# Hyena butterflies in a two-layer hybrid encoder: filter transforms on VectorE and in the attention, the convolution begun beside the queries

## The chip, the core and the metric

The kernel runs on one core of one Trainium2 chip, in one launch. The metric is device microseconds from start to end of the program. A profiled execution gives, besides its time, a trace of every engine: TensorE (PE, with its weight loads as PEld), VectorE (DVE), ScalarE (ACT), GpSimd (POOL) and the queue of SyncE (SP), which only issues transfers.

## What is computed

The reference is an encoder of two layers on 1024 tokens of width 1024, in float32. Each layer has a token mixer, a cross-attention into 256 memory tokens and a mixture of 16 experts, each with its residual and LayerNorm. The change lies in the mixer, whose three groups share one input projection:

```python
def hybrid_mix(x, ...):
    proj = x @ w_in
    gq, gk, gv, hy_u, c_q, c_kv, k_r = jnp.split(proj, IN_SPLITS, axis=-1)
    ...
    out_a = blocked_attention(q, k, v, HEAD_DIM ** -0.5)       # 8 heads, 2 key heads
    ...
    x0, x1, hv = jnp.split(short_conv3(hy_u, hy_cw, hy_cb), 3, axis=-1)
    filt = hyena_filters(n_tok, ...)                           # from weights alone
    out_b = x0 * bidir_long_conv(hv * x1, filt, hy_bias)
    ...
    out_c = blocked_attention(q_c, k_c, v_c, ...)              # latent attention, 4 heads
    return jnp.concatenate([out_a, out_b, out_c], axis=-1) @ w_o

def bidir_long_conv(z, h, bias):
    zs = jnp.fft.rfft(z, n=2 * n_tok, axis=1)
    fs = jnp.fft.rfft(filt_circ, axis=0)
    y = jnp.fft.irfft(zs * fs, n=2 * n_tok, axis=1)[:, :n_tok]
    return y + z * bias
```

The filter's spectrum `fs` hangs on weights only; `zs` and `y` hang on the tokens.

## The kernel before, in words

Every product of two f32 matrices is made of three matmuls (`mm3`, L184 to L189) on operands split into a high and a low part: `split` (L173 to L176) lets ACT copy the high part (L175) and VectorE, or with `"p"` GpSimd, subtract the low part (L176). Work in SBUF goes through one pool of 41 buffers of 128x1024 f32 (`big`); PSUM has the pools S (two of 128x1024), T and O (two of 128x512 each). The orders of PE, ACT and DVE are those in which the program text issues the instructions; a scheduler orders the queues of GpSimd and SyncE. The program text interleaves generators with `next()`, and each `yield` is a place where another stream goes on.

A length-2048 real Fourier transform is made of matmuls with DFT tables (128x1024 of one residue class at a time) and of radix butterflies: sums and differences of whole 128x1024 or half 128x512 tiles, here named bf, then the four spectra (F of the filter, Z of the tokens, G of the product on its way back).

- `filter_spectra` (from L810) makes the filter spectra of **both** layers, at the start of the program: windows and DFT matmuls first, whose results are seven tiles X per layer (U and V), then butterflies (L908 to L918) and `radix` (L926 to L950, an operation itself at L931), which take VectorE and GpSimd in turn (`alt`), ScalarE's scaling of Q (L932) between them; each layer's four F are stored to DRAM (fd, L923). Its steps are pulled by `fill`, four to each of the eight latent tiles of layer 1's projection.
- That stretch of the projection (`in_proj`, called the latent stretch below) has 8 tiles of 24 matmuls of 416 columns into PSUM O, with weights wi split on ACT and DVE. Behind each tile VectorE has a few small operations (L373 to L375 the norm, L502, L508 and L510 the rotary part of the key); L508 is the last that reads the tile from PSUM.
- Then come six tiles of convolution inputs, the keys and values, and eight query tiles (the query stretch), with L466 the query transposes. Attention overlaps the last of them.
- `hyena` (L952 to L1077) is the convolution. It reloads the tokens' channels, makes four transposes (T, L974) and four DFT steps (D), the forward butterflies (L994 to L997 and `radix`), four products with F (L1010 to L1017), the inverse butterflies (L1024 to L1032 and `radix`), splits the four G with the low part abl on GpSimd (L1046 with L176), and runs the inverse DFT matmuls, transposes (L1057) and the gating. All its butterflies and products are GpSimd's. It takes its first step at projection step 18, and then one per attention iteration, for n = 3 to 57.
- `attention` has 96 iterations, two for each of 48 pairs of head and block: 64 of grouped-query attention, 32 of latent attention. In each PE makes scores S (L526), VectorE the row maximum (L529), ACT the exponentials (L535), PE transposes (L543), which ACT and VectorE split into PH and PL (L175, L176), and PE the output (L553, L554). After every second iteration ACT evicts olo (L565 to L567), of which there are two buffers, and GpSimd finishes it (L568, L569). `side(n, 2)` pulls the steps of other streams.

```python
            def side(n, at):
                ...
                if HY0 <= n < 58:
                    next(hy, None)
```

Of the kernel before, what the change touches and what calls it, by code (L numbers as in the profile page):

```python
# [11 lines left out]
F32 = mybir.dt.float32  # L12
# [7 lines left out]
D = 1024  # L20
# [12 lines left out]
TAIL = 88  # L33
ML0 = 1
FM = 14
HY0 = 3
AT0 = 14
UC = 1
UG = 3
# [98 lines left out]
class Net:  # L138
# [58 lines left out]
    def consts(self):  # L197
        nc, cp, A = self.nc, self.cp, self.A
        self.ident = cp.tile([128, 128], F32, name="ident")
        nc.sync.dma_start(self.ident, A["k_ident"])  # L200
        self.eps = cp.tile([128, 2], F32, name="eps")
        nc.vector.memset(self.eps[:, 0:1], 1e-6)
        nc.vector.memset(self.eps[:, 1:2], 1e-5)
        self.x1d = [self.dp.tile([N, D], F32, name=f"x1d{l}") for l in range(DEPTH)]
        self.x2d = [self.dp.tile([N, D], F32, name=f"x2d{l}") for l in range(DEPTH)]
        self.yd = [self.dp.tile([N, D], F32, name=f"yd{l}") for l in range(DEPTH)]
        self.x3d = self.dp.tile([N, D], F32, name="x3d")
        self.cd = [self.dp.tile([N, C_COLS], F32, name=f"cd{l}") for l in range(DEPTH)]
        self.kvd = [self.dp.tile([8, 128, 1024], F32, name=f"kvd{l}") for l in range(DEPTH)]
        self.ld = [self.dp.tile([20, 128, 1024], F32, name=f"ld{l}") for l in range(DEPTH)]  # L210
        self.zd = [self.dp.tile([4, 128, 1024], F32, name=f"zd{l}") for l in range(DEPTH)]
        self.fd = [self.dp.tile([4, 128, 1024], F32, name=f"fd{l}") for l in range(DEPTH)]

    def tables(self):
# [595 lines left out]
    def filter_spectra(self):  # L810
# [74 lines left out]
        for n in range(9):  # L885
# [18 lines left out]
            if n % 2 == 0 and n < 8:  # L904
                tab = nxt.pop()
                if n < 6:
                    nxt.append(self.table("k_dft", n // 2 + 1))
        for l in range(DEPTH):  # L908
            E, O, D, Od, Oe, Dd, Q = (self.big(sh, name="bf") for _ in range(7))
            u, v = U[l], V[l]  # L910
            for k, (o, a, b, op) in enumerate((
                    (E, u[0], u[1], OP.add), (O, u[2], u[3], OP.add), (Od, u[2], u[3], OP.subtract),
                    (Oe, v[1], v[2], OP.add), (Dd, v[1], v[2], OP.subtract),
                    (D[:, 0], u[0][:, 0], u[1][:, 0], OP.subtract), (D[:, 1], v[0][:, 0], v[0][:, 1], OP.subtract),
                    (Q[:, 0], Od[:, 0], Od[:, 1], OP.subtract), (Q[:, 1], Dd[:, 0], Dd[:, 1], OP.add))):
                self.alt().tensor_tensor(o, a, b, op)
                if k in (1, 3, 5, 8):
                    yield  # L918
            U[l] = V[l] = u = v = None
            F = [self.big(sh, name="F") for _ in range(4)]  # L920
            yield from self.radix(F, E, O, (Oe[:, 0], Oe[:, 1]), D, Q)
            for i in range(4):
                nc.sync.dma_start(self.fd[l][i], F[i].rearrange("p a b c -> p (a b c)"))  # L923
            yield

    def radix(self, F, E, O, b2, D, Q, pool=False):  # L926

        nc = self.nc  # L930
        tt = lambda *x: (nc.gpsimd if pool else self.alt()).tensor_tensor(*x)  # L931
        nc.scalar.activation(Q, Q, AF.Copy, scale=math.sqrt(0.5))  # L932
        S, AB = (self.big((128, 2, 2, 256), name="bf") for _ in range(2))
        tt(S[:, 0], E[:, 0], E[:, 1], OP.add)
        tt(S[:, 1], O[:, 0], O[:, 1], OP.add)
        yield
        tt(AB[:, 0], E[:, 0], E[:, 1], OP.subtract)
        tt(AB[:, 1], *b2, OP.subtract)
        yield
        tt(F[0][:, 0], S[:, 0], S[:, 1], OP.add)  # L940
        tt(F[0][:, 1], S[:, 0], S[:, 1], OP.subtract)
        yield
        tt(E, D, Q, OP.add)
        yield
        tt(O, D, Q, OP.subtract)
        yield
        for f, x in zip(F[1:], (AB, E, O)):
            for i, op in enumerate((OP.add, OP.subtract)):
                tt(f[:, i], x[:, 0], x[:, 1, ::-1], op)
            yield  # L950

    def hyena(self, l):  # L952
# [44 lines left out]
        tt(Q[:, 1], Od[:, 0], Od[:, 1], OP.add)  # L997
        del X[:]
        yield
        Z = [self.big(sh, name="Z") for _ in range(4)]  # L1000
        yield from self.radix(Z, E, O, (O[:, 0], O[:, 1]), D, Q, True)
        Y = []
        for i in range(4):
            F = self.big(sh, name="F")
            nc.sync.dma_start(F, self.fd[l][i].rearrange("p (a b c) -> p a b c", a=2, b=2))
            t1 = self.big(sh, name="y1")
            t2 = self.big(sh, name="y2")
            d = slice(None, None, -1 if i else 1)
            z, z2 = Z[i], t1[:, d, 1]
            tt(t1, z, F, OP.mult)  # L1010
            yield
            tt(t2[:, :, 0], z[:, :, 0], F[:, d, 1], OP.mult)
            tt(t2[:, :, 1], z[:, d, 1], F[:, :, 0], OP.mult)
            yield
            y = self.big(sh, name="y3")
            tt(y[:, :, 0], t1[:, :, 0], z2, OP.subtract)
            tt(y[:, :, 1], t2[:, :, 0], t2[:, :, 1], OP.add)  # L1017
            Y.append(y)
            yield
# [12 lines left out]
        tt(Q[:, 1], Od[:, 1], Od[:, 0], OP.subtract)  # L1032
        del Y
        yield
        G = [self.big(sh, name="G") for _ in range(4)]
        yield from self.radix(G, E, O, (O[:, 1], O[:, 0]), D, Q, True)
        for j in (4, 5):
            self.mix_dst(j * 128, 0, 1)
        zv = [reload(2 + i) for i in range(2)]
# [2 lines left out]
        for n in range(6):  # L1042
            if n < 4:
                ah = self.big(sh, F32R, name="abh")
                al = self.big(sh, F32R, name="abl")
                self.split(ah, al, G[n], "p")  # L1046
                tab = nxt.pop()
                if n < 3:
                    nxt.append(self.table("k_idft", n + 1))
                ready.append((n, ah, al, tab))  # L1050
                yield
            if late:
                q, t = late.pop()
                pt = self.psT((128, 2, 2, 128))
                for i in range(2):
                    for ct in range(2):
                        nc.tensor.transpose(pt[:, i, ct, :], t[:, i, ct * 128:ct * 128 + 128], self.ident)  # L1057
                a, b = INV[q]
                for ct in range(2):
                    for hf in range(2):  # L1060
                        s = slice(hf * 64, hf * 64 + 64)
                        w = slice(min(a, b), max(a, b) + 1, abs(b - a))
                        p = pt[:, :, ct, s] if a < b else pt[:, ::-1, ct, s]
                        dst = self.mix[hf][2][:, ct, :].rearrange("p (m r) -> p r m", r=8)[:, w, :]
                        nc.vector.tensor_tensor(dst, p, zv[ct][:, w, s], OP.mult)
                if n == 5:
                    yield
            if 0 < n < 5:
                q, ah, al, tab = ready.pop(0)
                P = self.psO((128, 2, 256))  # L1070
                for i in range(2):
                    for cs in range(2):
                        k = (i, cs) if q == 0 else (i ^ cs, cs)
                        self.mm3(P[:, i, :], tab[:, 0, i, cs, :], tab[:, 1, i, cs, :], ah[:, k[0], k[1], :], al[:, k[0], k[1], :], cs == 0, cs == 1)
                t = self.tmp((128, 2, 256), name="yt")
                nc.scalar.activation(t, P, AF.Copy)
                late.append((q, t))  # L1077
                yield
# [627 lines left out]
    def run(self):  # L1706
# [38 lines left out]
        for l in range(DEPTH):  # L1745
# [3 lines left out]
            wo = []  # L1749
            gqa, (mla, back) = self.gqa(), self.mla(l)  # L1750
            hy = self.hyena(l)

            def side(n, at):
                if at != 2:
                    return
                if HY0 <= n < 58:
                    next(hy, None)
                if n == 58:
                    drain(hy)
                if 57 <= n < 64 or n in (70, 78, 86):  # L1760
                    next(back, None)
                if n in (84, 86, 88, 90, 92, 94, 96, 97):
                    wo.extend(self.out_weights(A["w_o"][l], [len(wo)]))
# [3 lines left out]
            for n, _ in enumerate(proj, NT if l else 0):  # L1767
                if n == NT - 1 + (l > 0):
                    drain(mem if l else fill)
                if n == 18:  # L1770
                    next(hy)
                if AT0 + NT + 2 <= n:
                    next(att)
                    next(att)
                    ATS += 2
# [12 lines left out]
            for n, _ in enumerate(att, ATS):  # L1788
                if n == PS:
                    next(pl)  # L1790
            if PS > 101:
                next(pl)
            T1 = self.new_T()
# [123 lines left out]
def drain(g):  # L1917
    for _ in g:
        pass
# [63 lines left out]
```

## Time and profile before

| | before |
|---|---|
| median of 3 runs (lowest to highest) | 2769.97 us (2769.33 to 2772.05) |
| the profiled execution's own time | 2770.48 us |
| its span, first to last instruction | 2768.7 us |
| mean granted TensorE clock | 0.967 of full |
| PE busy | 2548.5 us, 92% |
| DVE busy | 1960.4 us, 71% |
| ACT busy | 1588.1 us, 57% |
| POOL busy | 872.8 us, 32% |

The two layers pass through the same stages, layer 2 some 1320 us behind layer 1; only the first has the filter's work. Layer 1's latent stretch lies at 135 to 195 us of the span, its grouped-query attention at 370 to 590, its latent attention at 590 to 693. A table of busy times by stretch of time is the way to read these stages apart: the shares over the whole span are averages of stages with different limits.

### The profile page before, as it was taken

To read this page: it belongs to the slowest core of one execution; us is meant where nothing else is said; L and a number is where in the kernel's file an instruction comes from. 1 tells how busy PE (TensorE), PEld (TensorE's weight loads), DVE (VectorE), ACT (ScalarE), POOL (GpSimd) and SP (SyncE) were. 2 spreads that over 40 slices of the span, in tenths; PEclk is the share of its full clock that TensorE was granted. 3 is DMA by queue.
4 is the path that set the end of the run, shared out by engine and by line. 5 is a ranking of instruction groups with operands and counts; after the bars stand their busy time and mean duration, and the time that the engine had idled before them with its cause. 6 is when DMAs were issued, how large, how long until landed. Compare 5 with 4: busy or idle time off the path is not lost. (4 is left out here: it accounts for less than half of the span.)

```text
span 2768.7 us, 39154 instructions
## 1 busy us (share of the span) xinstructions
PE 2548.5 (92%) x14132; PEld 2146.8 (78%) x14132; DVE 1960.4 (71%) x3066; ACT 1588.1 (57%) x2828; POOL 872.8 (32%) x784
## 2 busy tenths in 40 slices
PE   7879999899899995999989998989989999599998
PEld 5668878789778884777769887878977887477775
DVE  6775568677653478888977456877766347888887
ACT  4624259788323443778854425977841344278885
POOL 2473339932301300111132333994230121011112
PEclk9889999999999997999999999999999999799999
DMA  7436100142232356999975620114223234699994
GB/s 200 145 133 214 52 24 32 43 103 77 84 106 79 106 181 237 333 372 377 345 258 175 192 75 24 31 39 107 69 91 107 77 99 160 252 327 371 379 350 152
DMA packets 220563, 455.40 MB, mean 164 GB/s; under 512 B 26074, under 2 KB 82992, under 8 KB 220370
## 3 DMA queue, kind: packets, MB, share of 16 engines
q1 hardware_dynamic: 196386, 367.22, 37.9%
q0 software_dynamic: 19376, 68.91, 9.3%
q10 hardware_dynamic: 4608, 16.78, 1.5%
q8 instruction: 111, 1.82, 0.3%
q14 instruction: 82, 0.67, 0.1%
HBM read 366.08 MB, written 86.77 MB: 164 GB/s over the span
## 5 line engine op out<-in xcount | busy, mean ns | idle before, releaser
L176 DVE TENSOR_TENSOR egl<-eg,egh 128x1024 fp32r<-128x1024 f32 x256 | 305.9, 1221 | 49.7 <-ACT egh L175 45.2
L529 DVE TENSOR_REDUCE nm<-S 128x1 f32<-128x1024 f32 x192 | 234.4, 1223 | 109.2 <-PE S L526 108.1
L175 ACT ACTIVATE egh<-eg 128x1024 fp32r<-128x1024 f32 x256 | 265.2, 1058 | 40.9 <-PE S L188 23.8
L176 DVE TENSOR_TENSOR PL<-T,PH 128x512 fp32r<-128x512 f32 x384 | 246.2, 683 | 40.5 <-ACT PH L175 38.2
L175 ACT ACTIVATE PH<-T 128x512 fp32r<-128x512 f32 x384 | 209.2, 595 | 76.5 <-PE T L543 75.5
L543 PE MATMUL T<-ident,E 128*128 128x128 f32 x1536 | 205.8, 276 | 18.5 <-DVE PL L176 17.7
L543 PEld LDWEIGHTS T<-ident,E 128*128 128x128 f32 x1536 | 181.1, 142 | 50.1 <-DVE PL L176 22.8
L535 ACT ACTIVATE E<-S,nm 128x1024 f32<-128x1024 f32 x192 | 214.6, 1118 | 7.5 <-DVE nm L529 7.4
L187 PE MATMUL S<-woh,mh 128*128 128x512 f32 x512 | 207.5, 405 | 6.3 <-DVE r L1150 6.3
L188 PE MATMUL S<-wol,mh 128*128 128x512 f32 x512 | 202.2, 395 | 3.6 <-POOL wol L176 2.4
L187 PE MATMUL S<-egh,xt 128*128 128x512 f32 x512 | 204.1, 399 | 0.0
L189 PE MATMUL S<-woh,ml 128*128 128x512 f32 x512 | 201.6, 394 | 0.0
L189 PE MATMUL S<-egh,xt 128*128 128x512 f32 x512 | 200.7, 392 | 0.0
L188 PE MATMUL S<-egl,xt 128*128 128x512 f32 x512 | 200.6, 392 | 0.0
L176 DVE TENSOR_TENSOR edl<-ed,edh 128x1024 fp32r<-128x1024 f32 x128 | 153.2, 1220 | 18.5 <-ACT edh L175 18.5
L1658 PE MATMUL O<-edh,ht 128*128 128x512 f32 x512 | 155.3, 406 | 1.4 <-ACT ht L175 1.4
L568 POOL TENSOR_TENSOR olo<-olo 64x256 f32<-64x256 f32 x96 | 70.0, 729 | 269.4 <-ACT olo L566 267.7
L526 PE MATMUL S<-KS,QS 128*128 128x512 f32 x512 | 148.8, 415 | 1.2 <-ACT E L535 1.2
L1600 POOL DMA_INDIRECT xg<-x2d,ix x32 | 54.6, 1705 | 301.2 <-PE O L1658 143.1
L175 ACT ACTIVATE edh<-ed 128x1024 fp32r<-128x1024 f32 x128 | 132.3, 1055 | 22.9 <-PE S L188 13.2
L553 PE MATMUL O<-PH,VS 128*128 128x256 f32 x512 | 139.3, 305 | 0.0
L1673 POOL DMA_INDIRECT yd<-ye,ix x31 | 49.0, 1582 | 260.8 <-DVE egl L176 114.0
(423 smaller groups left out, 7148.8 us busy)
## 6 DMA issues: line engine op xcount, KB each, us to landing
eg<-moe_w_gate SPq DMA_DIRECT2D x128, 512.0 KB, 10.9
eg<-moe_w_up SPq DMA_DIRECT2D x128, 512.0 KB, 11.0
ed<-moe_w_down SPq DMA_DIRECT2D x128, 512.0 KB, 11.3
wv<-xa_wkv SPq DMA_DIRECT2D x16, 512.0 KB, 8.1
wk<-xa_wkv SPq DMA_DIRECT2D x16, 512.0 KB, 6.3
wo<-w_o SPq DMA_DIRECT2D x16, 512.0 KB, 3.5
x1d<-r SPq DMA_DIRECT2D x16, 512.0 KB, 2.6
wq<-xa_wq SPq DMA_DIRECT2D x16, 512.0 KB, 4.0
```

Source lines behind the costliest of these rows:

```text
L175: self.nc.scalar.activation(h, src, AF.Copy)
L176: (self.nc.vector if le == "v" else self.nc.gpsimd).tensor_sub(l, src, h.bitcast(F32))
L187: mm(out, ah, bh, start=start, stop=False)
L188: mm(out, ah, bl, start=False, stop=False)
L189: mm(out, al, bh, start=False, stop=stop)
L526: self.nc.tensor.matmul(S[:, hf * 512:hf * 512 + 512], a, b[hf], start=n == 0, stop=n == len(passes) - 1)
L529: self.nc.vector.tensor_reduce(nm, S, axis=AX.X, op=OP.max, negate=True)
L535: self.nc.scalar.activation(E, S, AF.Exp, bias=nm, scale=1.0, accum_out=den)
L543: self.nc.tensor.transpose(pt[:, k, :], P[:, kt * 128:(kt + 1) * 128], self.ident)
L553: nc.tensor.matmul(O[:, :256], v, PH[half][:, k, :], start=kt == 0, stop=False)
L568: nc.gpsimd.tensor_tensor(lo[s, 0], lo[s, 0], lo[s, 1], OP.add)
L1658: nc.tensor.matmul(O[e][n], a[:, 2 * u + f, :], w[:, n * 512:n * 512 + 512], start=s, stop=z)
```

## The change

Four things are done, and PE's instructions stay the same in number.

1. Layer 1's filter butterflies run in the latent stretch as before, but all on VectorE (`filter_radix` with `nc.vector`), with two yields a step.
2. Layer 2's seven X tiles are stored to DRAM (ud, 512 KB each) by SP, right after the DFT. In layer 1's latent attention, at odd n over 62, `filter_later` loads them back and makes the butterflies on GpSimd: 7 operations on 128x1024 and 16 on 128x512, one scaling on ACT, four stores to fd.
3. The convolution takes a step at each projection step from 18 to 26, which is beside the queries, and then one at each attention iteration below 58 save each sixth.
4. The low parts of the four inverse splits go from GpSimd to VectorE. `radix` now makes and hands on one spectrum at a time, and frees its inputs earlier.

```diff
-HY0 = 3
+        self.ud = self.dp.tile([7, 128, 1024], F32, name="ud")
...
+        for i, x in enumerate(U[1] + V[1]):
+            nc.sync.dma_start(self.ud[i], x.rearrange("p a b c -> p (a b c)"))
+        uv = dict(enumerate(U[0] + V[0]))
+        del U, V, x
+        for _ in self.filter_radix(0, uv.pop, nc.vector):
+            yield
+            yield
+
+    def filter_later(self):
...
+        xs = {i: load(i) for i in (2, 3)}
...
+        yield from self.filter_radix(1, get, self.nc.gpsimd)
+
+    def filter_radix(self, l, get, eng):
+        tt, sh = eng.tensor_tensor, (128, 2, 2, 256)
+        def two(i, j):
+            a, b = get(i), get(j)
+            o = self.big(sh, name="bf")
+            tt(o, a, b, OP.add)
+            yield
+            tt(a, a, b, OP.subtract)
+            yield
+            return o, a
...
-                self.split(ah, al, G[n], "p")
+                self.split(ah, al, G.pop(n))
...
+            later = self.filter_later()
...
-                if HY0 <= n < 58:
+                if n < 58 and n % 6 != 5:
                     next(hy, None)
                 if n == 58:
                     drain(hy)
+                if n > 62 and n % 2 and l == 0:
+                    next(later, None)
...
-                if n == 18:
+                if 18 <= n:
                     next(hy)
```

On VectorE, at the start of the latent stretch, the rows before are these (bf are butterfly tiles, X the DFT's results, cn and r the latent tile's norm and rotary part):

```order
L878 COPY X<-S 128x512
L176 TENSOR_TENSOR xl<-T,xh 128x2x256
L916 TENSOR_TENSOR bf<-X 128x1024 x3
L916 TENSOR_TENSOR bf<-X 128x512
L916 TENSOR_TENSOR bf<-bf 128x512
L373 RECIPROCAL ri<-sd 128x2
L375 SCALAR_TENSOR_TENSOR cn<-O,ri,mgq 128x256
```

and with the change:

```order
L942 TENSOR_TENSOR bf<-X 128x1024
L944 TENSOR_TENSOR X<-X 128x1024
L373 RECIPROCAL ri<-sd 128x2
L375 SCALAR_TENSOR_TENSOR cn<-O,ri,mgq 128x256
L375 SCALAR_TENSOR_TENSOR cn<-O,ri,mgk 128x128
L502 TENSOR_TENSOR r_1272<-O,rope_369 128x32
L508 TENSOR_TENSOR r_1274<-O,rope_369 128x2x8 x2
L510 TENSOR_TENSOR cn<-r_1272,r_1274 128x32
L942 TENSOR_TENSOR bf<-X 128x1024
L944 TENSOR_TENSOR X<-X 128x1024
```

Where five butterflies stood ahead of the first tile's norm, and others on GpSimd beside them, two stand ahead of it and two to four behind each tile, and none on GpSimd.

On GpSimd, from the end of the query stretch into the attention, the rows before (tab are DFT tables, t and xr the queries' rotary part):

```order
L287 TENSOR_TENSOR t_3226<-xn,rg 128x16x16 x2
L292 TENSOR_TENSOR xr<-xr,t_3226 128x512
L803 DMA tab<-k_dft 128x1024 x3
L568 TENSOR_TENSOR olo<-olo 64x256
L569 TENSOR_TENSOR mix<-olo 64x256
L568 TENSOR_TENSOR olo<-olo 64x256
L569 TENSOR_TENSOR mix<-olo 64x256
L568 TENSOR_TENSOR olo<-olo 64x256
L569 TENSOR_TENSOR mix<-olo 64x256
L994 TENSOR_TENSOR bf<-X 128x1024 x2
```

and with the change:

```order
L803 DMA tab<-k_dft 128x1024
L287 TENSOR_TENSOR t_3169<-xn,rg 128x16x16 x2
L292 TENSOR_TENSOR xr<-xr,t_3169 128x512
L287 TENSOR_TENSOR t_3236<-xn,rg 128x16x16 x2
L292 TENSOR_TENSOR xr<-xr,t_3236 128x512
L1042 TENSOR_TENSOR bf<-X 128x1024 x4
L1044 TENSOR_TENSOR bf<-bf 128x512
L1045 TENSOR_TENSOR bf<-bf 128x512
L978 TENSOR_TENSOR bf<-bf 128x512
L979 TENSOR_TENSOR bf<-bf 128x512
L568 TENSOR_TENSOR olo<-olo 64x256
```

The convolution's eight first operations stand ahead of the first eviction pair now, where the first two stood behind the third pair.

In SP's queue ahead of the latent stretch, before:

```order
L820 DMA dec<-hy_decay 128x512
L826 DMA hyb<-hy_bias 1x512
L1243 DMA kvd_88<-kk 128x1024 x2
L1739 DMA x<-x 128x1024 x8
L127 DMA wi<-w_in 128x2x416 x4
L377 DMA cd_86<-cn 128x416
L923 DMA fd_94<-F 128x1024
L647 DMA c<-cd_86 128x416
```

and with the change:

```order
L820 DMA dec<-hy_decay 128x512
L826 DMA hyb<-hy_bias 1x512
L1293 DMA kvd_88<-kk 128x1024 x2
L1789 DMA x<-x 128x1024 x4
L909 DMA ud<-X 128x1024
L1789 DMA x<-x 128x1024 x4
L909 DMA ud<-X 128x1024 x4
L126 DMA wi<-w_in 128x2x416 x4
L909 DMA ud<-X 128x1024 x2
```

Five of the seven stores stand ahead of the latent weights wi, and wait for their X tiles there.

## Rows read from the trace of the kernel before

**Rows 1.** Busy time by stretch: start:end, length, then each engine, clock, DMA.

```profile
135.00:195.00 60.00, 44.94 (x194) 41.87 (x194) 53.24 (x76) 14.81 (x49) 46.22 (x24) 0.86 0.38 128
369.00:412.00 43.00, 38.00 (x237) 32.91 (x238) 30.49 (x41) 28.60 (x54) 7.17 (x10) 0.88 0.11 37
...
502.00:520.00 18.00, 11.03 (x66) 9.53 (x65) 8.15 (x13) 10.85 (x22) 17.53 (x15) 0.81 0.00 0
520.00:560.00 40.00, 35.27 (x260) 32.21 (x258) 28.75 (x42) 34.34 (x69) 32.23 (x29) 1.00 0.26 80
...
590.00:693.00 103.00, 103.00 (x714) 93.47 (x713) 76.11 (x108) 83.47 (x171) 24.88 (x36) 1.00 0.24 71
```

**Rows 2.** The same view, of L529 alone: one row maximum per attention iteration.

```profile
457.00:502.00 45.00, 19.58 (x16) 1.00 0.07 25
502.00:520.00 18.00, 3.65 (x3) 0.81 0.00 0
520.00:560.00 40.00, 13.47 (x11) 1.00 0.26 80
```

**Rows 3.** Timeline of the latent stretch: start, length, instruction, [idle before, releaser].

```profile
140.15 0.35 PE L189 MATMUL O<-wih,xl 128*128 128x416 f32 x1
140.34 0.36 PE L187 MATMUL O<-wih,xh 128*128 128x416 f32 x1
...
149.41 0.69 PE L187 MATMUL O<-wih,xh 128*128 128x416 f32 x1 [4.93 <-DVE r L508]
```

**Rows 4.** Groups of DVE and of POOL, 135 to 195 us: count, busy, mean ns, idle.

```profile
L931 DVE TENSOR_TENSOR F<-bf 128x512 f32<-128x512 f32 x8 | 12.8, 1631 | 0.0
L510 DVE TENSOR_TENSOR cn<-r,r 128x32 f32<-128x32 f32 x7 | 6.1, 868 | 0.2
L375 DVE SCALAR_TENSOR_TENSOR cn<-O,ri,mgq 128x256 f32<-128x256 f32 x7 | 3.4, 484 | 0.7
L375 DVE SCALAR_TENSOR_TENSOR cn<-O,ri,mgk 128x128 f32<-128x128 f32 x7 | 2.4, 342 | 0.0
L931 DVE TENSOR_TENSOR bf<-bf 128x1024 f32<-128x1024 f32 x2 | 2.4, 1213 | 0.0
L508 DVE TENSOR_TENSOR r<-O,rope 128x16 f32<-128x16 f32 x14 | 1.7, 165 | 0.0
...
L916 POOL TENSOR_TENSOR bf<-X 128x1024 f32<-128x1024 f32 x5 | 13.7, 2752 | 10.9 <-issue 6.4 <-DVE bf L916 4.5
```

**Rows 5.** Groups of DVE in layer 2, 1450 to 1560 us, without butterflies.

```profile
L510 DVE TENSOR_TENSOR cn<-r,r 128x32 f32<-128x32 f32 x8 | 1.5, 192 | 0.3
```

**Rows 6.** Timeline ahead of the latent stretch: SP's, ACT's and DVE's queues.

```profile
115.94 3.66 SPq L127 DMA_DIRECT2D wi<-w_in  x4
...
123.70 0.89 ACT L175 ACTIVATE wih<-wi 128x832 fp32r<-128x832 f32 x1
...
120.49 0.68 DVE L878 COPY X<-S 128x512 f32<-128x512 f32 x1
```

**Rows 7.** Groups of POOL in the attention, 412 to 560 us.

```profile
L568 POOL TENSOR_TENSOR olo<-olo 64x256 f32<-64x256 f32 x22 | 16.1, 733 | 8.6 <-ACT olo L566 7.7
...
L931 POOL TENSOR_TENSOR Z<-bf 128x512 f32<-128x512 f32 x8 | 10.1, 1287 | 0.1
...
L931 POOL TENSOR_TENSOR bf<-bf 128x1024 f32<-128x1024 f32 x4 | 9.5, 2398 | 0.0
```

**Rows 8.** Timeline of POOL: the convolution's first butterflies.

```profile
415.10 4.73 POOL L994 TENSOR_TENSOR bf<-X 128x1024 f32<-128x1024 f32 x2
```

**Rows 9.** Timeline of ACT and of PE, later in the attention.

```profile
510.99 1.06 ACT L932 ACTIVATE bf<-bf 128x1024 f32<-128x1024 f32 x1 [5.58 <-POOL bf L1032]
...
542.62 0.36 PE L187 MATMUL O<-abh,tab 128*128 128x256 f32 x1 [2.56 <-ACT E L535]
```

**Rows 10.** Groups of DVE: 505 to 560 us, then 590 to 693.

```profile
L176 DVE TENSOR_TENSOR PL<-T,PH 128x512 fp32r<-128x512 f32 x28 | 18.1, 685 | 11.2 <-ACT PH L175 11.0
...
L176 DVE TENSOR_TENSOR PL<-T,PH 128x512 fp32r<-128x512 f32 x62 | 39.6, 681 | 0.0
```

More of the change, by code (lines that the diff above doesn't have):

```diff
@@ L907, in filter_spectra @@
                     nxt.append(self.table("k_dft", n // 2 + 1))
[L908 to L923, printed above, removed]
-            yield
@@ L926, in radix @@
[L926 to L933, printed above, removed]
+        for i, x in enumerate(U[1] + V[1]):
[3 more added lines that the diff above has]
+        for _ in self.filter_radix(0, uv.pop, nc.vector):
+            yield
+            yield
@@ new lines, in filter_later, with load, get @@
+    def filter_later(self):
+        def load(i):
+            x = self.big((128, 2, 2, 256), name="X")
+            self.nc.sync.dma_start(x, self.ud[i].rearrange("p (a b c) -> p a b c", a=2, b=2))
+            return x
+        xs = {i: load(i) for i in (2, 3)}
+        def get(i):
+            order = (2, 3, 5, 6, 0, 1, 4)
+            for j in order[:min(7, order.index(i) + 3)]:
+                if j not in xs:
+                    xs[j] = load(j)
+            x, xs[i] = xs[i], None
+            return x
+        yield from self.filter_radix(1, get, self.nc.gpsimd)
@@ new lines, in filter_radix, with store @@
+    def filter_radix(self, l, get, eng):
[8 more added lines that the diff above has]
+            return o, a
+        O, Od = yield from two(2, 3)
+        Oe, Dd = yield from two(5, 6)
+        Q = self.big(sh, name="bf")
+        tt(Q[:, 0], Od[:, 0], Od[:, 1], OP.subtract)
+        tt(Q[:, 1], Dd[:, 0], Dd[:, 1], OP.add)
+        del Od, Dd
+        yield
+        u, w = get(0), get(1)
+        E, D = self.big(sh, name="bf"), self.big(sh, name="bf")
+        tt(E, u, w, OP.add)
+        yield
+        tt(D[:, 0], u[:, 0], w[:, 0], OP.subtract)
+        del u, w
+        w = get(4)
+        tt(D[:, 1], w[:, 0], w[:, 1], OP.subtract)
+        del w
+        yield
+        def store(i, f):
+            self.nc.sync.dma_start(self.fd[l][i], f.rearrange("p a b c -> p (a b c)"))
+        yield from self.radix(store, E, O, Oe, (0, 1), D, Q, tt)
@@ L934, in radix @@
+    def radix(self, emit, E, O, Oe, b2, D, Q, tt):
+        sh = (128, 2, 2, 256)
+        self.nc.scalar.activation(Q, Q, AF.Copy, scale=math.sqrt(0.5))
+        S, AB = (self.big(sh, name="bf") for _ in range(2))
         tt(S[:, 0], E[:, 0], E[:, 1], OP.add)
@@ L937, in radix @@
         tt(AB[:, 0], E[:, 0], E[:, 1], OP.subtract)
[L938 to L941, printed above, removed]
+        tt(AB[:, 1], Oe[:, b2[0]], Oe[:, b2[1]], OP.subtract)
         yield
@@ L946, in radix @@
         yield
-        for f, x in zip(F[1:], (AB, E, O)):
+        f = self.big(sh, name="Z")
+        tt(f[:, 0], S[:, 0], S[:, 1], OP.add)
+        tt(f[:, 1], S[:, 0], S[:, 1], OP.subtract)
+        emit(0, f)
+        yield
+        for n, x in enumerate((AB, E, O)):
+            f = self.big(sh, name="Z")
             for i, op in enumerate((OP.add, OP.subtract)):
                 tt(f[:, i], x[:, 0], x[:, 1, ::-1], op)
+            emit(n + 1, f)
             yield
@@ L999, in hyena @@
         yield
-        Z = [self.big(sh, name="Z") for _ in range(4)]
-        yield from self.radix(Z, E, O, (O[:, 0], O[:, 1]), D, Q, True)
+        Z = {}
+        yield from self.radix(Z.__setitem__, E, O, O, (0, 1), D, Q, tt)
+        del E, O, D, Od, Q
         Y = []
@@ L1008, in hyena @@
             d = slice(None, None, -1 if i else 1)
-            z, z2 = Z[i], t1[:, d, 1]
+            z, z2 = Z.pop(i), t1[:, d, 1]
             tt(t1, z, F, OP.mult)
@@ L1034, in hyena @@
         yield
-        G = [self.big(sh, name="G") for _ in range(4)]
-        yield from self.radix(G, E, O, (O[:, 1], O[:, 0]), D, Q, True)
+        G = {}
+        yield from self.radix(G.__setitem__, E, O, O, (1, 0), D, Q, tt)
+        del E, O, D, Od, Q
         for j in (4, 5):
@@ L1790, in run @@
                     next(pl)
+            if l == 0:
+                drain(later)
             if PS > 101:
```

## The prediction

> **What bounds the kernel now.** I read the busy times by stretch first. TensorE sets the pace where it is busy throughout: in the latent attention, 590 to 693 us, it works 103.00 of 103 us, and nothing there can be won [rows 1]. It does not set it in four other stretches of layer 1 [rows 1]: the latent stretch (44.94 of 60 us busy, at 0.86 of the clock), the start of attention (38.00 of 43, 0.88), the 18 us from 502 (11.03, 0.81) and the 40 us from 520 (35.27). The timeline says who is late. In the latent stretch it is VectorE: PE stands 4.93 us for L508, the last read of a PSUM tile [rows 3], which queues behind butterflies. Their lengths by group show why: with both engines at it, a 128x512 butterfly takes VectorE 1.63 us, an addition of 32 columns 0.87, and a 128x1024 takes GpSimd 2.75 [rows 4]; in layer 2, without butterflies, the same 32 columns take 0.19 [rows 5]. In attention it is GpSimd: it is busy 17.53 of the 18 us from 502 [rows 1], and ACT stands 5.58 us with the scaling of Q, behind L1032 [rows 9]; everything after it in ACT's order, the exponentials among it, stands too.
>
> **Latent stretch, layer 1.** At full clock the matmuls follow each other in 0.19 us (140.15 to 140.34) [rows 3]. Eight tiles of 24 make 192 x 0.19 = 36.5 us; the stretch lasts 60.0, so at most 23.5 can go, stalls and half clock together. VectorE's work afterwards, all butterflies included: 7 x 1.21 [rows 4] and 16 of 128x512, for which I take the 0.68 that this size costs in attention [rows 10], 19.4 us or 2.4 a tile; its own operations 0.48 + 0.34 + 2 x 0.165 [rows 4] + 0.19 [rows 5], with two smaller ones some 1.7. Together 4.1 us, under PE's 4.56: PE becomes the bound, by a small margin. GpSimd has nothing left there, so nothing slows VectorE. Two things take from the 23.5. The weights wi are now issued behind five stores of X, of which the last waits for the copy that ends at 121.2; they were issued at 115.94 and first split at 123.70 [rows 6]. If they need all of those 7.8 us, the first split moves by 5.3; if they land sooner, by less, at the least by nothing. I take 3. For clock and hand-overs left I take 1.5. Gain 19, between 12 and 23.5.
>
> **Convolution in attention, both layers.** PE's steady pace is 16 iterations in 45 us, 2.81 each [rows 2]. The 18 us from 502 hold 3 iterations [rows 2], so 18 - 8.4 = 9.6 us are lost. They are a backlog: forward butterflies (14 x 1.29 + 6 x 2.40 = 32.5 us), products (4 x (2.40 + 4 x 1.29) = 30.2) and the inverse's first ones (some 12.5) by the lengths in [rows 7], with an eviction pair of 2 x 0.73 [rows 7] per two iterations (34 iterations, 25), make 100 us; GpSimd has 96 from its start at 415.10 [rows 8] to the end of the stall at 510.99 [rows 9]. With the change these steps begin some 40 us earlier (the first DFTs are beside the queries) and take five of six iterations: 41 iterations or 115 us for the same work plus pairs, 105. GpSimd is then in time, and the 9.6 go.
>
> At the start of attention PE idles 5.0 of 43 us and loses clock besides [rows 1]; five of the eight transpose and DFT steps leave it. Their PE work only moves, so I count 3 (0 to 5). In the 40 us from 520, PE idles 4.73 [rows 1]; one wait there is 2.56 before the first inverse DFT [rows 9]. The trace names the exponentials, but these were done; the other operand is the low part abl, which GpSimd makes. With abl on VectorE and the steps earlier I take 3.5 of the 4.73 (0 to 4.7).
>
> The moved low parts cost VectorE 4 x 1.21, and it has 40 - 28.75 = 11.25 us free there [rows 1], which hides them; if each also waits for a GpSimd operation of 2.40 [rows 7], as butterflies did in the latent stretch, it is 9.6 more, 3.2 over what is free. I take 1 (0 to 9.6). So a layer gives 9.6 + 3 + 3.5 - 1 = 15, and two 30, between 12 and 38. Layer 2 has the same PE work and nothing of the filter's.
>
> **Rule against row.** VectorE's PL, which reads one operand from PSUM, takes 0.685 us beside a busy GpSimd and 0.681 beside a mostly idle one [rows 10], whereas the butterflies with both operands in SBUF suffer [rows 4]. The Trainium skill, GPSIMD Engine Reference, section "1. Specifications", says that GpSimd shares its SBUF interfaces with VectorE, and that instructions of VectorE with two SBUF inputs contend. By that rule the low parts on VectorE, two SBUF inputs each, would contend every time, and the sum would be smaller by up to 17 us; the trace agrees with the rule on butterflies and on PL, and shows no low part on VectorE beside GpSimd.
>
> **Layer 2's filter, moved into layer 1's latent attention.** GpSimd gets 16 x 1.29 + 7 x 2.40 = 37.5 us [rows 7] on top of 24.88 in 103 us [rows 1]: room is ample. VectorE's work there is PL and maxima, both from PSUM, and is not slowed [rows 10]. The seven stores and loads of 512 KB and the four stores of F cost by what queues behind them: loads of latent-attention keys on GpSimd's queue behind a butterfly that waits for a load, output weights on SP's behind the stores, and ACT and VectorE tiles that take a buffer last held by a butterfly or a load. I count about a dozen such places. At nothing each they cost nothing; at the 2.56 of the wait in [rows 9] 31 us. PE has no slack in this stretch, but most of these buffers come free an iteration early. I take 3.
>
> **Sum.** 2770.5 (the profiled execution's own time) - 19 - 30 + 3 = 2724.5. That execution lies 0.5 over the median, so the forecast is 2724.
>
> **Rivals.**
> - *Attention only swaps its wait.* GpSimd's work in time lets ACT, 34.34 of 40 us busy from 520 [rows 1], or VectorE become late, or the last transpose and DFT steps, now between the first scores, queue with them for PSUM. Half of the 30 goes: 2739; all: 2754. For it speaks the small slack of ACT, against it that PE is full at the same ACT load before 502. Chance 0.15.
> - *The latent stretch stays bound by VectorE or starts late.* 4.1 against 4.56 us a tile is thin; one butterfly of 1.2 us late per tile (8 x 1.2 = 9.6) and wi at the full 5.3 leave 8 to 9 of the 19: 2735. Chance 0.13.
> - *The low parts meet GpSimd every time.* Both layers pay 9.6 instead of 1: 2724 + 17 = 2741. GpSimd has few operations left when the inverse DFT begins, and VectorE has slack, which speaks against it. Chance 0.08.
> - *Slower.* The latent attention of layer 1 loses more than the rest gives. It decides where the dozen waits on butterfly buffers, loads and stores cost over 4 us each: 49 + 6 us, 2776 or more. PE's 103.00 of 103 [rows 1] means that each comes through in full; but a load is issued two steps, four iterations, ahead. Chance 0.04.
> - *No change to be measured.* The rows of the order show that the parts do move, so this needs gains and costs that cancel. Chance 0.05.
>
> **How the numbers follow.** The forecast and small deviations from it (2705 to 2733) have 0.55. The upper end of the range takes in the first three rivals, 2754; the lower is the ceiling of the parts: 23.5 + 38 with no cost gives 2708, with layer 1's further waits at the start some 2704. Left out are slower, no change, and a remainder, under 0.2 together. Some 0.2% or 5.5 us is what a measurement of this kernel tells from no change. Faster by more than that: 0.91; within: 0.05; slower: 0.04.
>
> **What would show it.** In the latent stretch PE should be busy over nine tenths, the 192 matmuls should take under 42 us, and VectorE's 128x1024 butterflies 1.2 us each. In attention the stall at Q's scaling should be gone, with 15 or 16 maxima in every 45 us, and PE idle under 2 us at the inverse DFTs. In the latent attention PE should stay above 100 of 103 us. If the latent stretch starts with PE waiting for wi, or if stalls name GpSimd or DMA between 590 and 693, the terms of 3 us were too small. The forecast is wrong altogether if the stretches from 502 to 560 keep their idle time in both layers.

## The result

The changed kernel takes 2752.33 us (median of 4, 2752.09 to 2754.91) against 2769.68 before: a ratio of 0.9938 (0.992 to 0.9955), faster by 17 us where 46 were forecast. The sign was right, and the size was not. The profiled execution is the slowest of the four; its span is 2753.1 us, 15.6 less than before.

Where the time went is read from one row that both kernels have 96 times a layer, the row maximum L529: how much earlier than before does the same iteration of attention start? With the start of the convolution inputs (L420) ahead of it, this gives the following, worked out from start times in the traces (us earlier than before; the columns e3 to e7 are experiments, told below):

```
                              changed   e3     e4     e5     e6     e7
layer 1  L420 begins             21.4  21.8   20.0   19.4   21.7   21.7
         iteration 0              9.5  21.6   14.1   13.5   14.4   21.7
         iteration 18            16.7  21.6   21.4   19.4   24.6   21.2
         iteration 45            25.3  18.5   29.9   28.0   32.9   20.2
         iteration 61            22.8  16.6   27.0   31.6   36.7   21.3
         iteration 95            13.8   8.0   18.3   31.6   36.7   21.3
layer 2  L420 begins             14.0   9.9   18.7   31.7   37.1   22.6
         iteration 0              4.0   9.9   12.8   25.8   29.8   22.6
         iteration 18            10.6   9.6   18.5   32.4   39.5   22.5
         iteration 45            19.0   5.8   27.0   40.8   47.6   22.5
         iteration 61            16.5   2.4   24.5   44.5   51.5   22.5
         iteration 95            16.5   2.4   24.5   44.5   51.5   22.4
```

Each column is one execution. Up to L420 of layer 1 the versions run the same program, and still its start differs by up to 2.4 us; so a stretch is read as a difference down a column, taken before rounding. In the first column the latent stretch gives 21.4. The queries then take 11.9 of it, and 7.2 come back by iteration 18, 4.7 lost in all; the stall around iteration 42 gives 8.6; the inverse takes 2.5; the latent attention takes 9.0. Layer 2 loses 9.9 in its queries, gets 6.6 back by iteration 18 and 8.4 at the stall, and loses 2.5 in its inverse.

**The latent stretch** is what the change made of it. Groups of VectorE from 110 to 175 us (count, busy, mean ns, idle before):

```profile
L996 DVE TENSOR_TENSOR Z<-bf 128x512 f32<-128x512 f32 x6 | 3.8, 688 | 0.0
...
L944 DVE TENSOR_TENSOR X<-X 128x1024 f32<-128x1024 f32 x2 | 2.4, 1224 | 0.1
```

With GpSimd idle the half-size butterfly takes 0.69 us instead of 1.63 [rows 4], and no wait for VectorE is left. The first latent matmul stands at 137.32, and L420 begins at 173.7: 36.4 us, PE's own time, as it is busy in all of them. Busy time of the window of [rows 1], in which PE was busy 44.94 us:

```profile
135.00:195.00 60.00, 59.21 (x305) 54.84 (x305) 40.26 (x96) 23.49 (x70) 7.08 (x14) 1.00 0.53 170
```

The weights are late, within the price. Timeline of SP and of ACT:

```profile
122.09 2.88 SPq L126 DMA_DIRECT2D wi<-w_in  x4
```
```profile
128.22 0.90 ACT L174 ACTIVATE wih<-wi 128x832 fp32r<-128x832 f32 x1 [3.94 <-DMA wi<-w_in]
```

The first split is 4.5 us later than in [rows 6], of which the latent matmuls' start shows 2.3.

**The stretches after it.** Busy time by stretch of the changed kernel, columns as in [rows 1]:

```profile
320.00:340.00 20.00, 16.22 (x68) 12.78 (x68) 7.61 (x13) 4.63 (x9) 6.92 (x7) 0.83 0.10 36
...
360.00:380.00 20.00, 13.47 (x76) 10.84 (x74) 13.22 (x15) 10.62 (x18) 16.35 (x10) 0.91 0.00 1
495.00:516.00 21.00, 18.48 (x132) 16.02 (x131) 14.85 (x20) 17.92 (x36) 9.62 (x13) 1.00 0.24 78
516.00:530.00 14.00, 9.94 (x73) 8.56 (x73) 11.25 (x18) 9.00 (x18) 1.46 (x2) 1.00 0.10 36
590.00:693.00 103.00, 94.68 (x630) 84.79 (x628) 69.79 (x100) 78.03 (x158) 53.34 (x53) 0.96 0.33 103
```

Three stretches have holes now: the queries (320 to 340), the inverse (495 to 530) and the latent attention, which ends at 679 here, so that part of the last window lies behind it. Who PE waits for, in the query stretch and the start of attention, 266 to 400 us (engine, line, releaser, us, times, longest):

```profile
PE T L466 <- DVE PL L175: 4.5, 1, 4.5
PE T L466 <- DVE zt L175: 3.8, 2, 1.9
PE S L526 <- DVE X L180: 1.7, 1, 1.7
```

Before, from 280 to 415 us, the wait for zt came once, and none for PL stood before a query transpose:

```profile
PE T L466 <- DVE qst L176: 2.8, 2, 2.1
PE T L974 <- DVE PL L176: 2.1, 2, 1.1
PE T L466 <- DVE zt L176: 0.9, 1, 0.9
```

The query transposes L466 wait for a PSUM tile T in which the convolution's transposes lie, until VectorE has made their low part zt. The timelines of VectorE and PE show one of these waits:

```profile
320.27 0.69 DVE L278 TENSOR_TENSOR xn<-O,ri 128x512 f32<-128x512 f32 x1
321.00 0.69 DVE L280 TENSOR_TENSOR xr<-xn,rg 128x512 f32<-128x512 f32 x1
321.61 0.68 DVE L175 TENSOR_TENSOR zt<-T,zt 128x512 fp32r<-128x512 f32 x1
```
```profile
322.35 0.66 PE L466 MATMUL T<-ident,qst 128*128 128x128 f32 x4 [1.90 <-DVE zt L175]
...
323.82 0.63 PE L186 MATMUL O<-wih,xh 128*128 128x512 f32 x1
324.25 0.63 PE L187 MATMUL O<-wil,xh 128*128 128x512 f32 x1
```

zt stands behind the query's norm and rotary, as the step was pulled behind the tile. PE stops for 1.9 us and then runs its next matmuls spaced 0.43 us (323.82 to 324.25) in place of 0.23, at the lower of its clock's two levels; the granted clock of 0.83 from 320 to 340, with two such waits, makes that by my estimate some 1.7 us more for each (20 x 0.17 / 2). Layer 2 has the same two waits, of 1.90 and 1.89 us, but the clock falls behind one of them only (0.91 over the 20 us from 1646.9), and its loss from L420 to iteration 0 is 2.0 us less.

In the inverse, the timelines of ACT and of VectorE:

```profile
503.26 1.05 ACT L174 ACTIVATE abh<-Z 128x1024 fp32r<-128x1024 f32 x1
```
```profile
504.33 1.22 DVE L175 TENSOR_TENSOR abl<-Z,abh 128x1024 fp32r<-128x1024 f32 x1 [1.02 <-ACT abh L174]
505.48 1.22 DVE L529 TENSOR_REDUCE nm<-S 128x1 f32<-128x1024 f32 x1
```

The low part takes 1.22 us and is not slowed, but VectorE idles 1.02 us for ACT's high part ahead of it, and the next row maximum stands behind both.

In the latent attention, PE's waits from 590 to 700 us, and GpSimd's timeline ahead of one of them:

```profile
PE S L526 <- DMA mq<-ld: 3.8, 2, 2.3
```
```profile
612.33 1.29 POOL L978 TENSOR_TENSOR bf<-bf 128x512 f32<-128x512 f32 x1
613.58 1.29 POOL L979 TENSOR_TENSOR bf<-bf 128x512 f32<-128x512 f32 x1
614.95 2.40 POOL L986 TENSOR_TENSOR bf<-bf 128x1024 f32<-128x1024 f32 x1
617.29 1.04 POOL L717 DMA_DIRECT2D mq<-ld  x2
```
```profile
621.38 1.96 PE L526 MATMUL S<-mk,mq 96*128 96x512 f32 x6 [2.33 <-DMA mq<-ld]
```

GpSimd's queue issues the loads of the latent queries (mq), and now issues them behind three of layer 2's butterflies.

### The profile page after: what moved, and what is told of

It reads as the page before. It is cut to its first block, busy times and chain, and to the rows that moved or that the text cites. A ratio compares the mean times of both kernels' runs of the same rounds, so it can differ in the third digit from the quotient of the medians.

```text
span 2753.1 us, 39174 instructions
## 1 busy us (share of the span) xinstructions
PE 2544.5 (92%) x14132; PEld 2142.1 (78%) x14132; DVE 1952.4 (71%) x3074; ACT 1586.9 (58%) x2828; POOL 842.5 (31%) x776
## 4 chain that ended last, share of the span: by engine, by line
PE 68%; DVE 13%; ACT 6%; issue 6%; DMA 4%; POOL 1%; SPq 0%; ACTq 0%; DVEq 0%; POOLq 0%
PE S L186 7%; PE S L187 7%; PE S L188 7%; PE S L526 6%; PE T L543 5%; PE O L1708 5%; PE O L188 5%; PE O L187 5%; PE O L186 5%; PE S L420 4%; PE O L554 3%; PE O L553 3%; DVE rk L1511 1%; DMA eg<-moe_w_gate 1%; PE T L1462 1%
## 5 line engine op out<-in xcount | busy, mean ns | idle before, releaser
L529 DVE TENSOR_REDUCE nm<-S 128x1 f32<-128x1024 f32 x192 | 234.7, 1223 | 110.9 <-PE S L526 109.6
L175 DVE TENSOR_TENSOR PL<-T,PH 128x512 fp32r<-128x512 f32 x384 | 246.5, 683 | 14.9 <-ACT PH L174 10.6
```

The costliest lines, as they stand in the source:

```text
L175: (self.nc.vector if le == "v" else self.nc.gpsimd).tensor_sub(l, src, h.bitcast(F32))
L529: self.nc.vector.tensor_reduce(nm, S, axis=AX.X, op=OP.max, negate=True)
```

## The experiments

Times stand beside runs of the kernel before on the same chip: 2771.0 us for the first four, 2770.5 for the last three. The changed kernel's 2752.3 stands beside 2769.7, so a difference between two versions is known to 1 or 2 us.

**e1, low parts back on GpSimd.**

```diff
-                self.split(ah, al, G.pop(n))
+                self.split(ah, al, G.pop(n), "p")
```

> The changed kernel with the low parts of the four inverse splits back on GpSimd. Theory: on VectorE each of them stands ahead of the next row maximum and waits for ACT's high part, and that chain is what keeps the inverse stretch (497 to 545 us of layer 1) some 17 us over its steady pace; GpSimd is busy only 9.62 of the 21 us from 495, so it makes them in time now. Then every one of the four iterations loses about 1 us less, 4 us a layer: 2744 us. Rival: the stretch is bound by the work of PE and ACT that the inverse adds, and the place of the low parts decides nothing: 2752 us, within 2.

Measured: 2740.9 us, ratio 0.9887 (0.9871 to 0.9904). From iteration 45 to 61 this version gains 3.7 us in layer 1 where the changed kernel loses 2.5; in layer 2 it gains 3.6 where that loses 2.5. Busy times by stretch, the two windows of above, and GpSimd's group:

```profile
495.00:516.00 21.00, 19.86 (x150) 18.00 (x149) 16.16 (x25) 19.00 (x37) 15.76 (x15) 1.00 0.25 76
516.00:530.00 14.00, 13.76 (x104) 12.46 (x102) 11.14 (x19) 11.96 (x24) 5.33 (x6) 1.00 0.15 40
```
```profile
L175 POOL TENSOR_TENSOR abl<-Z,abh 128x1024 fp32r<-128x1024 f32 x4 | 9.6, 2390 | 3.7 <-DVE nm L529 1.9 <-ACT abh L174 1.7
```

PE works 13.76 of 14 us where it worked 9.94. A low part of 2.39 us on GpSimd is better than one of 1.22 on VectorE, which holds a row maximum up. The theory holds, and its size was too small: 6 us a layer, not 4.

**e2, the latent queries' loads earlier.**

```diff
-                if 57 <= n < 64 or n in (70, 78, 86):
+                if 57 <= n < 64 or n in (68, 76, 84):
```

> The changed kernel with the latent attention's query loads mq pulled at n = 68, 76 and 84 in place of 70, 78 and 86. Theory: the two stalls of layer 1's latent attention (2.33 us before a score at 621.38, its like at 652) are late mq loads, which stand on GpSimd's queue behind butterflies; issued two iterations earlier they land in time, the four long iterations (6.12, 5.03, 6.11, 5.00 us) go back to 3.3, and some 9 us come back: 2743.5 us. Rival: the buffers that filter tiles hold are what is short, so the loads wait for a buffer wherever they stand and the stalls stay: 2752 us.

Measured: 2744.1 us, ratio 0.9904 (0.9887 to 0.9921). No wait for mq is left. Busy times by stretch:

```profile
590.00:640.00 50.00, 50.00 (x347) 45.27 (x346) 36.88 (x53) 41.49 (x84) 32.14 (x33) 1.00 0.20 54
640.00:672.00 32.00, 32.00 (x225) 29.04 (x223) 23.83 (x34) 26.09 (x54) 15.97 (x17) 1.00 0.53 175
```

From iteration 61 to 95 it keeps its 23.0 us, where the changed kernel falls from 22.8 to 13.8. All of the 9 us came of two late loads; the other buffers that filter tiles share cost nothing here.

**e3, the convolution late again.**

```diff
-                if 18 <= n:
+                if n == 18:
                     next(hy)
...
-                if n < 58 and n % 6 != 5:
+                if n < 58:
                     next(hy, None)
```

> The changed kernel with the convolution's steps where they were: one at projection step 18, then one per attention iteration, none left out. Theory: beside the queries the steps cost 11.9 us in layer 1 and 9.8 in layer 2 and give back 5 at the start of attention; late, the stall at Q's scaling returns with about 8 us a layer. 2752 - 22 + 10 + 16 = 2756 us, and the latent stretch keeps its gain. Rival: the stall at Q's scaling went because radix frees its tiles earlier, not because of the earlier begin; then it stays away and the time is near 2740 us.

Measured: 2768.2 us (median of 10), ratio 0.9991 (0.9982 to 1.0001): 12 more than expected. From L420 to iteration 18 it loses 0.2 and 0.3 us, where the change loses 4.7 and 3.4; that is the early begin's net cost, less than the theory's 7 and 5. Then the stall at Q's scaling is back, and longer than before: to iteration 45 it loses 3.1 and 3.9 us against the kernel before, where the change gains 8.6 and 8.4. ACT's waits from 400 to 600 us:

```profile
ACT bf L976 <- POOL bf L1081: 9.1, 1, 9.1
```

Before it was 5.58 [rows 9]. This version takes the convolution's steps from iteration 0, not 3. Counted from iteration 18, ACT comes to the scaling 10.4 us sooner than before; GpSimd begins its butterflies 13.3 us sooner, but has finished what the scaling needs only 6.9 us sooner. e7 below takes the steps from 3 and has 5.6. The rival, that the early freeing of tiles removed the stall, falls. Which of two things removed it is not shown: e3 takes back both the early begin and the pause at each sixth iteration. The trace of the changed kernel speaks for both being needed: GpSimd is busy 56.94 of the 60 us from 400, and its L1081 ends at 470.26, only 1.5 us before the scaling at 471.71.

**e4, the steps in mid tile.** `mid` pulls the steps for the query tiles 4 to 9 of the loop; the steps from projection step 24 on stay where they were.

```diff
                     if k % 2 == 0:
                         next(parts, None)
+                    if k == 5:
+                        self.mid(n)
                     go(wq, P, n - 2, [k])
...
+            self.mid = lambda n, hy=hy: next(hy) if 4 <= n <= 9 else None
...
-                if 18 <= n:
+                if 24 <= n:
                     next(hy)
```

> The changed kernel with the six steps of the convolution beside the queries taken in the middle of a query tile (before its sixth eighth) in place of behind its rotary part. Theory: the loss in the query stretch is the wait of the query transposes for the PSUM tile of the convolution's transposes, whose low part zt stands on VectorE behind the query's norm and rotary operations (two waits of 1.9 us, each with nine matmuls at the half clock behind it); in mid tile VectorE is idle, and these waits go: 3.8 us idle and some 3 us of half clock a layer, 2739 us. Rival: what the moved matmuls and transposes themselves take of PE is the loss, wherever they stand: 2752 us.

Measured: 2744.1 us, ratio 0.99 (0.9883 to 0.9916), 8.3 of the 13 us expected. The two waits for zt are gone, and the stretch that had lost its clock is whole:

```profile
320.00:340.00 20.00, 19.77 (x107) 16.33 (x107) 12.04 (x19) 6.01 (x12) 9.25 (x10) 1.00 0.19 57
```

From L420 to iteration 0 this version loses 5.9 us in each layer, where the change loses 11.9 and 9.9. So the waits, with the clock lost behind them, are about half in layer 1 and less in layer 2. The rival holds for much of the rest: the five moved steps alone take PE by my estimate some 4.2 us (two DFT steps of 12 matmuls spaced 0.12, three transposing steps of 0.45). Waits of PE from 255 to 400 us, or the first two of them:

```profile
PE T L466 <- DVE PL L175: 3.5, 1, 3.5
PE S L528 <- DVE X L180: 2.3, 1, 2.3
```

**e5, the three edits together.** The edits of e1, e2 and e4.

> The changed kernel with three edits together: low parts of the inverse on GpSimd, query loads pulled at n = 68, 76 and 84, and the convolution's six steps in mid tile. Theory: the three losses lie in different stretches (inverse, latent attention, queries) and do not overlap, so the gains of the three single runs (11.4, 8.2 and 8.3 us) add: 2752.3 - 28 = 2724 us. Rival: they share a bound, one wait taking another's place, and less than two thirds of the sum comes: 2734 us or more.

Measured: 2723.8 us, ratio 0.9832 (0.9816 to 0.9849). The gains add: the three losses lie apart.

**e6, two tiles earlier.** As e5, with one number changed, which also puts the convolution two steps ahead from there on:

```diff
-            self.mid = lambda n, hy=hy: next(hy) if 4 <= n <= 9 else None
+            self.mid = lambda n, hy=hy: next(hy) if 2 <= n <= 9 else None
```

> As e5_three_mended, with the steps in mid tile begun two query tiles earlier, so that eight of the nine steps stand beside queries and only the last DFT step between the first scores. Theory: of the 7 us that the query stretch of layer 1 still loses in e4, two waits (3.5 us for PSUM T behind PL, 2.3 us for PSUM S behind X) come of transposes and DFT steps between the first scores; they go, 4 to 6 us a layer, 2714 us. Rival: what is left is the matmuls' own time, which only moves: 2724 us as e5, within 3.

Measured: 2719.6 us, ratio 0.9819 (0.9803 to 0.9836), the fastest version here. It is 4.2 us under e5, less than half of the 10 that the theory gave, and more than the rival allowed. By iteration 18 it has gained 2.9 and 2.4 us since L420, where e5 has gained 0.1 and 0.7. Waits of PE from 255 to 400 us:

```profile
PE T L466 <- DVE PL L175: 5.1, 1, 5.1
PE S L528 <- ACT E L537: 1.3, 1, 1.3
```

The wait for X has fallen to 0.4 us, and that of the last query's transposes for T behind PL stayed, at 5.1 us, although seven of the eight transpose and DFT steps now stand ahead of the scores. What it comes of was not tried.

**e7, the filter's part alone.** The convolution's steps at 18 and n = 3 to 57, low parts on GpSimd, loads as in e2; `radix` stays as changed.

```diff
-                if 18 <= n:
+                if n == 18:
                     next(hy)
...
-                if n < 58 and n % 6 != 5:
+                if 3 <= n < 58:
                     next(hy, None)
...
-                if 57 <= n < 64 or n in (70, 78, 86):
+                if 57 <= n < 64 or n in (68, 76, 84):
...
-                self.split(ah, al, G.pop(n))
+                self.split(ah, al, G.pop(n), "p")
```

> Only the filter's part of the change: layer 1's butterflies on VectorE, layer 2's in the latent attention, with the query loads at n = 68, 76 and 84; the convolution's steps at step 18 and n = 3 to 57 as before, low parts on GpSimd. Theory: the latent stretch's 21 us are kept to the end, as nothing else differs: 2750 us on a chip where the kernel before takes 2771. Rival: part of them was won only because the convolution no longer follows so late, or layer 1's attention gives it back on butterfly buffers: 2757 us or more.

Measured: 2751.0 us, ratio 0.9934 (0.9917 to 0.995). It is 21.7 us ahead at layer 1's first iteration and 22.4 at layer 2's last, so the latent stretch's gain is kept, as the theory had it. The filter's part, with its loads mended, gives at least as much as the whole change did (16.5 there; by the medians 19.4 against 17.3, which lie within each other's intervals). The convolution's part as it was written adds little: in the changed kernel's trace 4.0 us in both layers, 17.0 at the stall less 8.0 from the queries to iteration 18 and 5.0 in the inverse. The two add to what e2 keeps, which is 26.5 us ahead at the same place. By the medians e2 lies 7.5 us ahead of e7, so the 4.0 is known to a few us only.

## Why the prediction was wrong

**Latent stretch: right.** Forecast 19, measured 21.4. PE is the bound at 36.4 us; VectorE's butterflies fell to the undisturbed lengths; wi was issued at 122.09 (121.2 or later was forecast). The Trainium skill's rule on the interfaces that GpSimd shares with VectorE (GPSIMD Engine Reference, section "1. Specifications") agrees with both traces of this stretch: L510 took 0.87 us beside GpSimd and 0.19 with it idle. It does not tell which of GpSimd's operations cost time; the last section has low parts that met GpSimd and were not slowed, and there the measurement decides.

**The stall at Q's scaling: right.** Forecast 9.6 a layer; the gain from iteration 18 to 45 is 8.6 and 8.4. e3 and e7, in which the stall is back, show that the new order of steps does it: the early begin together with the pauses, as the prediction counted them, not parted.

**The start of attention: the step that failed most.** It was priced at +3 a layer, with the remark that the moved PE work "only moves". Measured to iteration 18: 16.7 - 21.4 = -4.7 in layer 1; in layer 2, 10.6 - 14.0 = -3.4. I looked for room on VectorE and PE in the query stretch and did not ask which buffer the moved transposes take: they share PSUM's two T tiles with the query transposes, and their release stands behind a norm and a rotary on VectorE. The prediction named this for the attention's first scores only, in a rival. With the steps in mid tile and two tiles earlier (e6) the same sum is 24.6 - 21.7 = +2.9 and 39.5 - 37.1 = +2.4: the +3 can be had, with the steps placed otherwise. What failed is that a move of PE's work was taken to cost nothing where it went.

**The inverse: wrong.** Forecast +3.5 - 1; measured -2.5 in each layer. By e1 that is +3.7 for the earlier steps and -6.2 for the low parts on VectorE, in place of -1. The +3.5 came out for another reason than the one given. The prediction laid the wait of 2.56 us before the first inverse DFT to abl; GpSimd's timeline of before shows that abl was done 1.0 us before PE went on at 542.62:

```profile
538.61 0.57 POOL L803 DMA_DIRECT2D tab<-k_idft  x1
539.25 2.35 POOL L176 TENSOR_TENSOR abl<-G,abh 128x1024 fp32r<-128x1024 f32 x1
```

What came last was the DFT table's load, ahead of it in the same queue: such loads land 3.9 us after their issue by the median, which is 542.5. In e1, with abl on GpSimd still but the steps earlier, PE does not wait there. The price of the low parts was sought in VectorE's busy time (11.25 us free) and in collisions with GpSimd. The collisions did not come, each of the four low parts took 1.22 or 1.23 us; so the rival of the shared port falls, as GpSimd had little left to do. What came was order: a low part waits for ACT's high part, and the row maximum behind it waits too. It is the first rival, an exchange of waits, in this stretch alone. The sum's lower end hid it: the ends of its terms (9.6 + 0 + 0 - 9.6) give nothing at all for a layer, but 12 was written for two. Measured were 4.0.

**Layer 2's filter in the latent attention: wrong by a factor of three.** Forecast 3, measured 9.0. The other buffers and loads cost nothing (e2). The one place that cost was on the list ("loads of latent-attention keys on GpSimd's queue behind a butterfly"), but as one of a dozen equal ones. It was two query loads behind 5.0 and 2.5 us of butterflies. That the loads had little to spare was to be seen in the trace of before, and I did not work it out: one pair is issued at 634.89, such loads land in 4.3 us by the median, so at 639.2 or later, and the row maximum of the scores that read them is at 643.23.

**Sum.** The profiled execution gained 15.6 us where 46.0 were forecast, 30.4 less. The terms give +2.4 (latent), -2.2 (stall), -14.0 (start of attention, both layers), -10.0 (inverse), -6.0 (loads) and -0.9 behind layer 2's attention, together -30.7. The last is no effect of the change that can be told: in that stretch the other versions, which do not differ there, lie between -1.0 and +0.5.

## What to carry to other kernels

When a step is moved to a stretch where every engine has room, price the buffers it shares there and the place of its release in the other engine's order, not only its work: here two PSUM tiles decided 4 to 6 us a layer, and half a tile's shift gave it back. Work put on an idle engine is free only for that engine; whatever stands behind it in the same order (a load, a row maximum) has to be followed to who waits for it. Where a trace names a releaser that was long done, look at every operand of the waiting instruction, loaded tables too. And a short operation on the engine in the chain can cost more than one twice as long on an engine outside it.

## What was not expected of the hardware

A wait of PE of 1.9 us cost about 3.6 where the granted clock fell behind it (above). In the latent attention two waits of 3.8 us in all made four iterations long (6.12, 5.03, 6.11 and 5.00 us in place of 3.33), 9.0 us together. From 590 to 679, where the attention ends, PE idles 4.8 us: the two loads, and 0.9 behind ACT's exponentials. Most of the rest is the clock: it is 0.89 of full from 615 to 630 and 0.90 from 645 to 662, by the estimate of above 1.7 us each.

Operations of VectorE with two SBUF operands did meet GpSimd beside the queries, and not all of them were slowed. Timelines of VectorE and of GpSimd at the start of attention:

```profile
359.04 0.68 DVE L175 TENSOR_TENSOR qst<-xr,qst 128x512 fp32r<-128x512 f32 x1
368.28 1.97 DVE L175 TENSOR_TENSOR qst<-xr,qst 128x512 fp32r<-128x512 f32 x1 [1.86 <-ACT qst L174]
```
```profile
357.87 2.44 POOL L287 TENSOR_TENSOR t<-xn,rg 128x256 f32<-128x256 f32 x2 [4.25 <-DVE xn L278]
367.32 5.13 POOL L1042 TENSOR_TENSOR bf<-X 128x1024 f32<-128x1024 f32 x2 [3.32 <-ACT X L182]
```

The query's low part took 0.68 us, its length with GpSimd idle, in the midst of GpSimd's rotary products L287, and 1.97 beside a forward butterfly. In the trace of before, five of the eight low parts of layer 1's queries stand beside L287 at 0.68, and one that ran into the addition L292 took 1.08. So the prediction was wrong that the trace of before shows no low part on VectorE beside GpSimd, and whether such a meeting costs time depended here on what GpSimd was doing. Why the products cost nothing was not tried.
